# Two sets of modulation dot products in a two-layer diffusion trunk: the latent tokens' change engines, the context's change stage

## The chip, the cores and the metric

The kernel runs on one core of one Trainium2 chip. The metric is the device time of one execution in microseconds (us). Three runs of the kernel before took 1449.05, 1447.75 and 1448.95 us; the median is 1448.95. Five engines work side by side, each through its own instruction queue in order: TensorE (PE, with its weight loads as PEld), VectorE (DVE), ScalarE (ACT), GpSimd (POOL) and SyncE (SP). SP issues all the transfers of this kernel.

## What is computed

There are 1024 latent tokens and 256 context tokens of 1024 numbers each, and two layers. Layer 0 is a windowed attention with grouped keys and values, layer 1 a neighbourhood attention on a grid. Every layer modulates its input with a scale and a shift and gates its output; scale, shift and gate come from a conditioning vector, one for the latent tokens (c) and another for the context (c_ctx).

```python
silu_c, silu_cc = jax.nn.silu(c), jax.nn.silu(c_ctx)
h, hc = x, ctx
for i in range(DEPTH):                        # DEPTH = 2
    shift, scale, gate = jnp.split(silu_c @ w_ada[i] + b_ada[i], 3, axis=-1)
    shift_c, scale_c, gate_c = jnp.split(silu_cc @ w_ada[i] + b_ada[i], 3, axis=-1)
    u = h * (1.0 + scale[:, None, :]) + shift[:, None, :]
    uc = hc * (1.0 + scale_c) + shift_c
    y, yc = mixer_a(...) if i == 0 else mixer_b(...)      # (o * silu(g)) @ w_out
    h = layer_norm(ALPHA * h + gate[:, None, :] * y, ln_g[i], ln_b[i])
    if i < DEPTH - 1:
        hc = layer_norm(ALPHA * hc + gate_c * yc, ln_g[i], ln_b[i])
return h
```

What the change touches are three products of a vector with a 1024 x 1024 matrix, for both vectors: the gate of layer 0 and the shift and scale of layer 1. They are needed only after the first attention: the gates when the output projection's result is gated, shift and scale when the second layer's input u is made.

## The kernel before, in words

**Stages.** Up to about 100 us the first layer's input is modulated and its keys and values are projected. From there to about 590 us the first attention runs over eight head pairs p (some 61 us each), with the projections of the same pair's gate path and the next pair's queries as filling between its steps. The output projection follows to about 697 us, with the first layer norm and the second layer's input, ten blocks b of 128 tokens (0 to 7 latent, 8 and 9 context). Then come the second layer's projections and attention and its output projection. Each float32 product is made of three matmuls on a high part (hi) and a low part (lo = value − hi) of both operands: hi is a cast on ScalarE, lo a subtraction on VectorE or GpSimd.

**The order of work.** The program is written as lists of pieces that `merge` puts together, attention steps with projection pieces. A list scheduler then orders every engine's queue: of the instructions that it takes to be ready it picks the one that stands first in the program. A tile with a tag takes one of the tag's buffers as one comes free; an instruction that needs a buffer waits for the last user of an older tile. `keep_in_program_order` pins an instruction behind the one written just before it for its engine.

**The dots (L592 to L634).** 48 pieces, `dot_half(h, j)` for half h of the 1024 inputs and group j of 128 outputs (j 0 to 7 gate, 8 to 15 shift, 16 to 23 scale), are put evenly into the steps of the first seven head pairs (`SEG`, L41; L819). A piece first gives ScalarE the previous piece's sum (`dot_sum`, pinned in program order). Then it loads 128 x 512 weights (tile gw, 256 KB, two buffers), multiplies and sums them with the latent vector in one VectorE instruction (L617, into the scratch tile gj, which has the tag ra, one buffer, together with the rotary evacuation and the gate's tanh), and multiplies them with the context's vector on GpSimd (L618), in place. That product's sum is the ScalarE instruction L599. Each half starts with both vectors spread over 128 partitions (gh), with silu made of a tanh on ScalarE and an operation on VectorE. `dots_end` (L623) adds the halves and the bias and makes colA and colB, the columns that turn the normalised z into u.

**The attention's tail (p = 7, L824 to L848).** The output projection's weights are loaded and split there (`wo_piece`, tags whi and wlo of the pool wp, four buffers each), block 0 is projected, and `gate_rows` spreads both gates over the partitions (eight transposes and one copy each, tile gates).

**The output projection (L854 to L918).** Before the loop `w.split(NA + 4)` (L858) loads the first four weight tiles of the second layer and splits them. A weight tile takes a raw buffer (wr, tag wraw, two buffers), and a hi and a lo buffer (tags whi and wlo). `og_load` takes the same two raw buffers for each block's attention output (ogr, two halves); `og_split` makes its hi on ScalarE (L385) and its lo on VectorE (L386). For block b the loop loads the residual z, splits og of b, loads ogr of b + 1, issues the block's 48 matmuls (yA), and then `u_from` of the block before: eight transposes of its z on TensorE (uT), eight operations on VectorE (ut, one buffer, two halves), the cast uBh on ScalarE (L887) and the subtraction uBl on GpSimd (L888). After that stand the gate product (L908), the residual (L909), statistics, the root on GpSimd (L429, rsd), and z on ScalarE (L915), which is stored (zdd, blocks 0 to 7) and transposed one block later. Behind the loop the second layer's projections begin (L942), with the weights that `w.split` has made and u of all eight latent blocks.

Of the kernel before, what the change touches and what calls it, by code (L numbers as in the profile page):

```python
# [43 lines left out]
def f32(ap):  # L44
    return ap.bitcast(F32)
# [37 lines left out]
def build(tc, i, out):  # L83
# [13 lines left out]
    def psbig(name):  # L97
        return ps.tile([P, 1024], F32, tag="big", bufs=2, name=name)
# [264 lines left out]
    def gate_rows(dst, src):  # L363

        pg = psbig("gate")
        for j in range(KT):
            nc.tensor.transpose(pg[:, j * P : (j + 1) * P], src[:, j : j + 1].to_broadcast([P, P]), ident)
        nc.scalar.copy(dst, pg)
# [222 lines left out]

    dhalf = cp.tile([P, 24, 2], F32, name="dhalf")  # L592
    gh, sums = [], []
# [7 lines left out]
    def dot_half(h, j):  # L601
        def run():
            dot_sum()
            if j == 0:
                gh.clear()
                for v in range(2):
                    t = px.tile([P, 512], F32, tag=f"gh{v}", bufs=1, name="gh")
                    dma(t, bass.AP(i["cr"].tensor, v * D + h * 512, [[0, P], [1, 512]]))
                    th = px.tile([P, 512], F32, tag="gw", bufs=2, name="gth")
                    nc.scalar.activation(th, t, AF.Tanh, scale=0.5)  # L610
                    nc.vector.scalar_tensor_tensor(t, th, 1.0, t, ALU.add, ALU.mult)
                    gh.append(t)
# [4 lines left out]
            nc.vector.tensor_tensor_reduce(o, t, gh[0], 0.5, 0.0, ALU.mult, ALU.add, accum_out=acc[:, j, 0:1])  # L617
            nc.gpsimd.tensor_tensor(t, t, gh[1], ALU.mult)  # L618
            sums.append((t, acc[:, j, 1:2]))

        return (0.0, run, 0)

    def dots_end():  # L623
        dot_sum()
        for v in range(2):
            d = dcol[:, 0:24, v]
            nc.vector.tensor_tensor(d, d, dhalf[:, 0:24, v], ALU.add)
            nc.vector.tensor_tensor(d, d, bad[:, 16:40], ALU.add)
            shift, scale = dcol[:, 8:16, v], dcol[:, 16:24, v]
            nc.vector.scalar_tensor_tensor(colA[:, v, :], scale, 1.0, lnc[:, 0, :], ALU.add, ALU.mult)  # L630
            nc.vector.scalar_tensor_tensor(colB[:, v, :], scale, 1.0, lnc[:, 1, :], ALU.add, ALU.mult)
            nc.vector.tensor_tensor(colB[:, v, :], colB[:, v, :], shift, ALU.add)

    dots = [dot_half(h, j) for h in range(2) for j in range(24)]  # L634
# [175 lines left out]
    for p in range(8):  # L810
# [6 lines left out]
        if p < 7:  # L817
# [3 lines left out]
            if not dots:  # L821
                att.append((0.0, dots_end, 0))
            merge(att, gprojA(p) + qprojA(p + 1), lead=0.0)
        else:  # L824
# [20 lines left out]
            for v in range(2):  # L845
                gate_rows(gts[:, v], dcol[:, 0:8, v])
# [11 lines left out]
    w.split(NA + 4)  # L858
# [30 lines left out]

    pend = None  # L890
    for b in range(10):
        z = oa.tile([P, D], F32, tag="z", bufs=2, name="z")
        dma(z, i["htok"][b])
        if b == 0:
            yh = yA0
        else:
            o = og_split(up, raw, "h2") if b % 2 else og_split(oa, raw, "og")
            if b < 9:
                raw = og_load(0, b + 1)
            y = psbig(f"yA{b}")  # L900
# [17 lines left out]
        pend = (b, z)  # L918

# [419 lines left out]
```

## Time and profile before

| what | value |
|---|---|
| median of three runs | 1448.95 us |
| the profiled execution | 1450.25 us |
| its span, first to last instruction | 1448.5 us |
| TensorE's granted clock | 0.994 |
| one gw load, from issue to landing | 2.8 us |
| tanh of gh on ScalarE, 4 times | 633 ns |
| bytes moved, over the whole span | 195 MB, 135 GB/s |

The profile is of one execution. A row of the timeline has start, duration, engine, line, operation, what it writes and reads, its size and, in brackets, how long the engine had been idle before it and which instruction released it. A row of a group has, behind the count, the busy time and the mean in nanoseconds, or the lowest, median and highest duration. A row of waits has who waited for whom, the microseconds in total, how many times, and the longest. A row of stretches has start and end, length, and each engine's busy time with its number of instructions, then the clock, the DMA share and GB/s. SPq rows are transfers as SP issues them; "landing" counts from issue to the data's arrival.

### The profile page before, as it was taken

The page shows a single profiled execution, that of the slowest core. Times are in us where ns is not written, and L with a number is a line of the kernel's source. Part 1 is how long each engine was busy: PE and PEld are TensorE (multiplying, and loading weights), DVE is VectorE, ACT ScalarE, POOL GpSimd, SP SyncE. Part 2 cuts the span into 40 slices and gives each one's busy share as a digit, 9 for nine tenths or more (in the row PEclk, how much of TensorE's full clock was granted, in tenths as well). Part 3 has the DMA queues.
Part 4 walks back from the last instruction along what each step waited for, and adds up shares of the span by engine and source line. Part 5 has one row for each costly group of instructions (what it writes and reads, how often), then busy time and mean ns, then how long its engine had stood idle before and what let it go on. Part 6 is the DMA issues. An engine that isn't in the chain of part 4 may idle for free. (4 is left out here: it accounts for less than half of the span.)

```text
span 1448.5 us, 25148 instructions
## 1 busy us (share of the span) xinstructions
PE 1393.6 (96%) x8815; PEld 1217.2 (84%) x8816; DVE 988.8 (68%) x2216; ACT 733.9 (51%) x1561; POOL 631.7 (44%) x779
## 2 busy tenths in 40 slices
PE   8998999999999999999999999999999999998995
PEld 5887888888888888788888899888988898887775
DVE  4658887878888789566423766555565565667698
ACT  4336776677676778332222545554454444557310
POOL 0326666666666657233301333333233333336664
PEclk9999999999999999999999999999999999999998
DMA  9472114123222124434278565565555564384353
GB/s 369 172 227 85 60 48 131 45 77 101 68 70 62 56 67 131 133 129 136 75 216 230 156 195 152 150 166 146 168 147 152 146 182 140 102 207 151 114 133 93
DMA packets 117229, 195.05 MB, mean 135 GB/s; under 512 B 9328, under 2 KB 57840, under 8 KB 117104
## 3 DMA queue, kind: packets, MB, share of 16 engines
q1 hardware_dynamic: 117104, 193.45, 44.4%
q8 instruction: 70, 1.15, 0.3%
q14 instruction: 55, 0.45, 0.1%
HBM read 141.51 MB, written 51.90 MB: 134 GB/s over the span
## 5 line engine op out<-in xcount | busy, mean ns | idle before, releaser
L329 POOL TENSOR_SCALAR s_B<-s_B,rs_B 128x640 f32<-128x640 f32 (+1 forms) x128 | 101.1, 790 | 298.0 <-DVE rs_B L328 243.9
L208 PE MATMUL pj<-uBh,wh 128*128 128x512 f32 (+1 forms) x448 | 176.0, 393 | 0.0
L209 PE MATMUL pj<-uBl,wh 128*128 128x512 f32 (+1 forms) x448 | 170.3, 380 | 0.0
L210 PE MATMUL pj<-uBh,wl 128*128 128x512 f32 (+1 forms) x448 | 170.1, 380 | 0.0
L324 ACT ACTIVATE s_B<-s_B,m_B 128x640 f32<-128x640 f32 (+1 forms) x128 | 102.9, 804 | 131.2 <-DVE m_B L317 131.1
L324 ACT ACTIVATE s_A<-s_A,m_A 128x641 f32<-128x641 f32 (+2 forms) x160 | 119.5, 747 | 88.7 <-DVE m_A L317 73.7
L164 POOL TENSOR_TENSOR wl<-wr,wh 128x512 fp32r<-128x512 f32 x64 | 87.7, 1370 | 162.1 <-ACT wh L162 139.8
L329 POOL TENSOR_SCALAR s_A<-s_A,rs_A 128x640 f32<-128x640 f32 (+2 forms) x160 | 126.8, 793 | 58.0 <-DVE rs_A L328 55.7
L317 DVE CUSTOM_DVE_ANT_0 s_A<-S_A,msk,nsk 128x640 f32<-128x640 f32 (+2 forms) x160 | 123.6, 774 | 34.1 <-PE S_A L705 17.7
L342 DVE TENSOR_TENSOR pt_B<-T_B,pt_B 128x640 fp32r<-128x640 f32 (+1 forms) x128 | 100.9, 788 | 61.0 <-ACT pt_B L340 60.6
L208 PE MATMUL pj<-uAh,wh 128*128 128x512 f32 (+1 forms) x384 | 140.0, 365 | 0.0
L209 PE MATMUL pj<-uAl,wh 128*128 128x512 f32 (+1 forms) x384 | 137.8, 359 | 0.0
L210 PE MATMUL pj<-uAh,wl 128*128 128x512 f32 (+1 forms) x384 | 137.5, 358 | 0.0
L342 DVE TENSOR_TENSOR ptl_A<-T_A,pth_A 128x640 fp32r<-128x640 f32 (+2 forms) x160 | 114.0, 713 | 15.3 <-PE pvA L733 7.1
L336 PE MATMUL T_A<-ident,s_A 128*128 128x128 f32 x672 | 101.1, 275 | 12.2 <-DVE m_A L317 8.9
L336 PEld LDWEIGHTS T_A<-ident,s_A 128*128 128x128 f32 x672 | 77.2, 140 | 40.2 <-issue 16.7
L340 ACT CAST pt_B<-T_B 128x640 fp32r<-128x640 f32 (+1 forms) x128 | 84.3, 658 | 47.6 <-PE T_B L336 46.6
L317 DVE CUSTOM_DVE_ANT_0 s_B<-S_B,bias 128x640 f32<-128x640 f32 (+1 forms) x128 | 100.4, 784 | 10.5 <-PE S_B L1036 9.7
L340 ACT CAST pth_A<-T_A 128x640 fp32r<-128x640 f32 (+2 forms) x160 | 96.4, 603 | 16.8 <-PE T_A L336 14.1
L210 PEld LDWEIGHTS pj<-uBh,wl 128*128 128x128 f32 x448 | 84.3, 188 | 16.6
L336 PE MATMUL T_B<-ident,s_B 128*128 128x128 f32 x608 | 88.7, 275 | 9.9 <-DVE pt_B L342 5.0
L242 PE MATMUL pv<-wh,uBh 128*128 128x256 f32 x320 | 92.8, 291 | 3.1 <-ACT wh L162 3.1
(219 smaller groups left out, 3883.6 us busy)
## 6 DMA issues: line engine op xcount, KB each, us to landing
kB<-kdB SPq DMA_DIRECT2D x64, 320.0 KB, 5.2
gw<-in_wadaT SPq DMA_DIRECT2D x48, 256.0 KB, 2.8
vdB<-st SPq DMA_DIRECT2D x20, 512.0 KB, 3.2
vB<-vdB SPq DMA_DIRECT2D x16, 640.0 KB, 4.7
wada<-in_wadaC SPq DMA_DIRECT2D x16, 512.0 KB, 9.6
kdB<-st SPq DMA_DIRECT2D x16, 512.0 KB, 3.0
qdB<-st SPq DMA_DIRECT2D x16, 512.0 KB, 3.5
qB<-qdB SPq DMA_DIRECT2D x32, 256.0 KB, 4.7
```

The source lines that it names most:

```text
L164: e.tensor_tensor(lo, r, f32(hi), ALU.subtract)
L208: mm(pt[:, :n], hi[:, sl], rh, start=kt == 0, stop=False)
L209: mm(pt[:, :n], hi[:, sl], rl, start=False, stop=False)
L210: mm(pt[:, :n], lo[:, sl], rh, start=False, stop=kt == KT - 1)
L242: mm(pt, lh, hi[:, sl], start=kt == 0, stop=False)
L317: nc.vector.tensor_tensor_reduce(outp, sc, in1, scale, init if init is not None else 3e38, ALU.add, ALU.min, accum_out=s.m)
L324: nc.scalar.activation(s.t[:, :n], s.t[:, :n], AF.Exp, bias=s.m, scale=-1.0, accum_out=s.sum)
L329: nc.gpsimd.tensor_scalar(s.t[:, : s.w], s.t[:, : s.w], s.rs, 1.0, ALU.mult, ALU.mult)
L336: nc.tensor.transpose(tp[:, k * P : (k + 1) * P], s.t[:, src * P : (src + 1) * P], ident)
L340: nc.scalar.copy(pt.hi[:, :n, hl, :], tv)
L342: nc.vector.tensor_tensor(pt.lo[:, :n, hl, :], tv, f32(pt.hi[:, :n, hl, :]), ALU.subtract)
```

## The change

The dots become one piece for each vector v. The latent vector's 48 (v = 0) stay at their places in the attention, but the product is made on GpSimd and the sum on ScalarE; the VectorE instruction and its scratch tile are gone. The context's 48 (v = 1) go into the output projection's loop: six at block 0, and for blocks 1 to 7 two ahead of each half of the block's matmuls and two behind its z. Their tiles come from the pool wp, the vector (gh) under the tag whi, the weights (and the tanh) under wlo. `dots_end` is called for the context's gates when 32 of the 48 are issued and for its shift and scale after the last. The context's gates are spread at the end of block 7, in two halves through one-bank PSUM tiles. `w.split(NA + 4)` moves from ahead of the loop to the beginning of block 8.

```diff
-    def dot_half(h, j):
-        def run():
-            dot_sum()
...
-            acc = dhalf if h else dcol
-            t = px.tile([P, 512], F32, tag="gw", bufs=2, name="gw")
-            dma(t, i["wadaT"][j, :, h * 512 : (h + 1) * 512])
-            o = ap_.tile([P, 512], F32, tag="ra", bufs=1, name="gj")
-            nc.vector.tensor_tensor_reduce(o, t, gh[0], 0.5, 0.0, ALU.mult, ALU.add, accum_out=acc[:, j, 0:1])
-            nc.gpsimd.tensor_tensor(t, t, gh[1], ALU.mult)
-            sums.append((t, acc[:, j, 1:2]))
+    def dot_half(pl, v, h, j):
+
+        dot_sum()
+        if (v, h) not in gh:
+            t = pl("gh", 1)
+            dma(t, bass.AP(i["cr"].tensor, v * D + h * 512, [[0, P], [1, 512]]))
+            th = pl("gw", 2)
+            nc.scalar.activation(th, t, AF.Tanh, scale=0.5)
+            nc.vector.scalar_tensor_tensor(t, th, 1.0, t, ALU.add, ALU.mult)
+            gh[v, h] = t
+        t = pl("gw", 2)
+        dma(t, i["wadaT"][j, :, h * 512 : (h + 1) * 512])
+        nc.gpsimd.tensor_tensor(t, t, gh[v, h], ALU.mult)
+        sums.append((t, (dhalf if h else dcol)[:, j, v : v + 1]))
...
-            for v in range(2):
-                gate_rows(gts[:, v], dcol[:, 0:8, v])
+            gate_rows(gts[:, 0], dcol[:, 0:8, 0])
...
-    w.split(NA + 4)
...
+    late = [(1, h, j) for h in range(2) for j in range(24)]
+
+    def late_tile(x, n):
+        return f32(wp.tile([P, 512], F32R, tag="whi" if x == "gh" else "wlo", bufs=4, name=x))
+
+    def late_dots(n):
+        for _ in range(n):
+            dot_half(late_tile, *late.pop(0))
+            if len(late) == 16:
+                dots_end(1, slice(0, 8))
+            elif not late:
+                dots_end(1, slice(8, 24))
+
     for b in range(10):
+        if b == 0:
+            late_dots(6)
+        elif b == 8:
+            w.split(NA + 4)
         z = oa.tile([P, D], F32, tag="z", bufs=2, name="z")
...
             for sl in HALVES:
+                if b < 8:
+                    late_dots(2)
                 out_part(yh, sl, o, woA, range(KT))
...
         pend = (b, z)
+        if 0 < b < 8:
+            late_dots(2)
+        if b == 7:
+            gate_rows(gts[:, 1], dcol[:, 0:8, 1], True)
```

More of the change, by code (lines that the diff above doesn't have):

```diff
@@ L361, in wo_piece, with gate_rows @@
         e.tensor_tensor(lo, r, f32(hi), ALU.subtract)
[L363 to L368, printed above, removed]
+    def gate_rows(dst, src, halves=False):
+        for n in range(2 if halves else 1):
+            pg = psone("gate") if halves else psbig("gate")
+            for j in range(KT // 2 if halves else KT):
+                k = KT // 2 * n + j
+                nc.tensor.transpose(pg[:, j * P : (j + 1) * P], src[:, k : k + 1].to_broadcast([P, P]), ident)
+            nc.scalar.copy(dst[:, HALVES[n]] if halves else dst, pg)
     def og_load(l, b, n=KT):
@@ L592, in build @@
     dhalf = cp.tile([P, 24, 2], F32, name="dhalf")
-    gh, sums = [], []
+    gh, sums = {}, []
     def dot_sum():
@@ L623, in dots_end @@
-    def dots_end():
-        dot_sum()
[L625 to L632, printed above, removed]
@@ L635, in build @@
+    dots = [(0.0, lambda h=h, j=j: dot_half(lambda x, n: px.tile([P, 512], F32, tag=x, bufs=n, name=x), 0, h, j), 0) for h in range(2) for j in range(24)]
     evs = []
@@ L821, in build @@
             if not dots:
-                att.append((0.0, dots_end, 0))
+                att.append((0.0, lambda: dots_end(0, slice(0, 24)), 0))
             merge(att, gprojA(p) + qprojA(p + 1), lead=0.0)
```

21 lines of the change are left out of this document (10 added, 11 removed).

## The prediction

> **What bounds the kernel now.** I read the page's engine shares first, then the busy time by stretches, then what TensorE waits for.
>
> ```profile
> span 1448.5 us, 25148 instructions
> PE 1393.6 (96%) x8815; PEld 1217.2 (84%) x8816; DVE 988.8 (68%) x2216; ACT 733.9 (51%) x1561; POOL 631.7 (44%) x779
> 222.00:283.00 61.00, 58.61 (x383) 51.09 (x382) 50.68 (x122) 42.94 (x99) 39.96 (x58) 1.00 0.26 81
> 600.00:697.00 97.00, 95.98 (x455) 79.30 (x456) 64.34 (x135) 30.22 (x55) 30.62 (x40) 1.00 0.38 125
> ```
>
> The third line is one head pair of the first attention (span, then PE, PEld, DVE, ACT, POOL), the fourth the output projection with its layer norm. TensorE is busy nearly throughout: 2.4 us idle in the 61, 1.0 in the 97. So time is gained only where TensorE waits, and any new wait of TensorE is paid in full. In the attention VectorE is the second engine (50.68 of 61, 83%); in the output projection GpSimd (30.62 of 97, 32%) and ScalarE (31%) have room. TensorE's waits while the dots run, 100 to 527 us:
>
> ```profile
> PE T_A L336 <- DVE m_A L317: 5.7, 11, 1.6
> PE S_A L704 <- DVE ptl_A L342: 5.1, 7, 1.2
> PE S_A L705 <- DVE ptl_A L342: 1.8, 6, 0.3
> PE T_A L336 <- POOL gw L618: 1.3, 1, 1.3
> ```
>
> Together 13.9 us, 12.6 of them on VectorE: that is all that a lighter VectorE can give in this stage.
>
> **The change part by part.** First, the latent dots leave VectorE (L617).
>
> ```profile
> L617 DVE CUSTOM_DVE_ANT_0 gj<-gw,gh 128x512 f32<-128x512 f32 x48 | 38.1, 794 | 1.4 <-DMA gw<-in_wadaT 1.0
> 249.21 1.52 DVE L617 CUSTOM_DVE_ANT_0 gj<-gw,gh 128x512 f32<-128x512 f32 x1 [0.46 <-DMA gw<-in_wadaT]
> 251.70 0.74 PE L336 MATMUL T_A<-ident,s_A 128*128 128x128 f32 x5 [1.16 <-DVE m_A L317]
> 372.24 1.46 DVE L617 CUSTOM_DVE_ANT_0 gj<-gw,gh 128x512 f32<-128x512 f32 x1 [0.53 <-DMA gw<-in_wadaT]
> 374.66 0.74 PE L336 MATMUL T_A<-ident,s_A 128*128 128x128 f32 x5 [1.16 <-DVE m_A L317]
> 125.29 0.74 PE L336 MATMUL T_A<-ident,s_A 128*128 128x128 f32 x5 [1.30 <-POOL gw L618]
> 280.34 0.39 PE L704 MATMUL S_A<-kA,qA 128*128 128x256 f32 x1 [0.67 <-DVE ptl_A L342]
> ```
>
> 48 reductions, 38.1 us of VectorE, go. GpSimd and ScalarE keep 48 products and 48 sums here, for the other vector. What TensorE gets back is far less than 38.1: the gaps at 251.70 and 374.66 stand right behind reductions of 1.52 and 1.46 us, and at 125.29 it waited for a product that itself waited for its reduction. That is 1.16 + 1.16 + 1.30 = 3.6 us for certain. Of the other 13.9 − 3.6 = 10.3 us I take the dots' share of VectorE's work, 38.1 in seven stretches of 50.68 (11%): 1.1. Gain 4.7 us; the bounds are 0 (work only leaves) and 13.9.
>
> Second, the context's 48 dots come into the output projection, each a load, a product on GpSimd and a sum on ScalarE:
>
> ```profile
> L618 POOL TENSOR_TENSOR gw<-gw,gh x48: 1262/1290/1306, 115.0 to 523.8; 128x512 f32<-128x512 f32 x48
> L599 ACT ACTIVATE gw<-gw x48: 613/632/648, 116.3 to 525.2; 128x512 f32<-128x512 f32 x48
> L599 ACT ACTIVATION_READ_ACCUMULATOR gw<-gw x48: 184/188/207, 116.8 to 525.7; 128x1 f32 x48
> ACT gw L599: 5.8, 9
> ```
>
> 48 × 1.29 = 62 us of GpSimd and 48 × 0.82 = 39 us of ScalarE. Six dots belong to each of blocks 0 to 7. The first ten (blocks 0 and 1, before the waits on block 1's normalisation) have the attention's tail for cover; if that is gone they join the queue below. A sum that waits for its product holds ScalarE's queue, the og casts and uBh behind it; in the attention that happened to 9 of 48, 5.8 us in all (last row), and ScalarE's 31% leaves room for it. The context's two tanh and their products, and the two VectorE steps that end its dots, move along; the last of these waits for dot 47's sum, with block 8's z behind it on VectorE, a microsecond that the wait ahead of block 9 (below) covers: nothing; 1 us if that wait is gone. One block's period, from one uBl to the next, with what stands in it:
>
> ```profile
> 675.45 1.44 POOL L888 TENSOR_TENSOR uBl<-ut,uBh 128x256 fp32r<-128x256 f32 x2 [5.23 <-ACT uBh L887]
> 678.81 1.90 POOL L888 TENSOR_TENSOR uBl<-ut,uBh 128x256 fp32r<-128x256 f32 x2 [1.92 <-ACT uBh L887]
> 681.47 0.55 POOL L429 TENSOR_TENSOR rsd<-rsd,half 128x1 f32<-128x1 f32 x1 [0.76 <-DVE rsd L428]
> 687.52 1.45 POOL L888 TENSOR_TENSOR uBl<-ut,uBh 128x256 fp32r<-128x256 f32 x2 [5.50 <-ACT uBh L887]
> 690.89 1.44 POOL L888 TENSOR_TENSOR uBl<-ut,uBh 128x256 fp32r<-128x256 f32 x2 [1.92 <-ACT uBh L887]
> 682.29 1.24 ACT L915 ACTIVATE z<-z,rsd 128x1024 f32<-128x1024 f32 x1 [3.25 <-issue]
> 684.30 1.04 PE L869 MATMUL uT<-ident,z 128*128 128x128 f32 x8
> 685.10 0.47 PE L419 MATMUL yA<-woAh,og 128*128 128x512 f32 x1
> 696.11 1.03 PE L869 MATMUL uT<-ident,z 128*128 128x128 f32 x8
> 679.40 0.70 DVE L386 TENSOR_TENSOR og<-ogr,og 128x512 fp32r<-128x512 f32 x1
> 680.14 1.11 DVE L386 TENSOR_TENSOR og<-ogr,og 128x512 fp32r<-128x512 f32 x1
> ```
>
> GpSimd has 1.44 + 1.90 + 0.55 = 3.9 us in a period of 12.07; six products add 7.74: 11.6, 96%. The chain from a block's last matmul to its transposes (uT) passes GpSimd twice, at the first uBl (the second half of ut has the same buffer) and at rsd; z ends at 683.53, 0.77 ahead of the transposes that read it. A product is in GpSimd's way 7.74/12.07 = 64% of the time and then by half of 1.29: 0.41 us a passage, 0.82 for two. That is about what the slack covers on average, so it costs something only when they bunch. In such a chain the loss is between 0 and, if two whole products stand in the way each time, 2 × 1.29 − 0.77 = 1.8 a block, 11 over blocks 2 to 7. I take 0.5 a block, 3 us, near the lower end: VectorE's statistics can be queued ahead of the late ut half.
>
> The second og subtraction took 1.11 where the first took 0.70, and it began while GpSimd's uBl was still running. The Trainium skill ("SBUF — State Buffer", SBUF: two separate sides) says that GpSimd and a VectorE operation with two SBUF inputs share one port pair, and whoever starts first shuts the other out for its whole instruction. These two rows agree. By that rule each product could also hold up the two og subtractions ahead of rsd.
>
> Third, the split of the second layer's first four weight tiles (four loads, casts, subtractions) moves from ahead of the loop to block 8. The rows of the raw buffers' queue:
>
> ```profile
> 571.36 2.55 SPq L148 DMA_DIRECT2D wr<-in_wBk  x2
> 576.71 0.33 SPq L148 DMA_DIRECT2D wr<-in_wBq  x1
> 578.48 0.33 SPq L148 DMA_DIRECT2D wr<-in_wBq  x1
> 581.30 3.67 SPq L375 DMA_DIRECT2D ogr<-ogd  x2
> 668.37 1.52 SPq L375 DMA_DIRECT2D ogr<-ogd  x2
> 672.47 1.14 ACT L385 CAST og<-ogr 128x512 fp32r<-128x512 f32 x2 [0.73 <-PE yA L421]
> DMA to landing us min/median/max: 2.5/2.9/6.3
> L162 ACT CAST wh<-wr x18: 604/620/625, 574.7 to 793.4; 128x512 fp32r<-128x512 f32 x18
> L164 POOL TENSOR_TENSOR wl<-wr,wh x9: 1285/1293/1298, 575.4 to 791.4; 128x512 fp32r<-128x512 f32 x9
> L164 DVE TENSOR_TENSOR wl<-wr,wh x9: 680/693/1369, 577.5 to 794.9; 128x512 fp32r<-128x512 f32 x9
> ```
>
> The tag wraw has two buffers, for wr and ogr alike, and they are given in program order: four wr, and only then the next block's ogr (581.30). Under the cover of the attention's tail that cost nothing. After the change the four wr stand between block 8's ogr and block 9's, which now loads at 668.37 for matmuls at 685.10. The pace of the old place (571.36 to 581.30, 9.9 us) would still do: 668.37 + 9.9 + 2.9 + 0.62 = 681.8. But a wr gives its buffer back only when its low half is written, and the low halves (wlo, four buffers) wait for the last dots to be summed. The sums of dots 45 and 46 are pinned behind block 7's z, that of 47 behind them. So: z ends at 683.53; the three sums end at 684.35, 685.17 and 685.99 (0.82 each). The third weight tile's low half on GpSimd then ends at 685.17 + 1.29 = 686.5 and frees the first buffer for ogr; it lands at 689.4 (2.9) and is cast by 690.0 (0.62). TensorE, which could start at 685.10, waits 4.9 us. The other half: 684.35 + 0.69 (VectorE) = 685.0, the fourth wr lands at 687.9, cast 688.6, low half 689.3, ogr 692.2, cast 692.8; the first half's twelve matmuls last until 690.0 + 12 × 0.23 = 692.8 (block 9's 48 take the 11.0 us from 685.10 to 696.11), so nothing more. Nothing else is ready for TensorE: the second layer's projection needs block 7's uBl, which ended at 690.89 + 1.44 = 692.3 even without the products. Cost 4.9; bounds 0 (as in the old place) and 4.9 + 3 × 1.29 = 8.8, if the last three products are late too.
>
> What moves at no cost: the context's gate rows (8 transposes and copies) go from the tail to block 7; TensorE does the same work. Each of the 48 loads is issued by the SP queue ahead of the ogr, z and zdd transfers there; at 38% DMA share, and with ogr loaded about 4 us (668.37 against the cast at 672.47) and its matmuls 17 us ahead, I take none of it.
>
> Sum, against the profiled execution's own 1450.25 us: − 4.7 + 3 + 4.9 = + 3.2, 1453.45. The median of the runs, 1448.95, lies 1.3 below that execution; the forecast is 1452.1 us. A measurement of this kernel tells about 0.2%, 2.9 us, from no change: this is just over it.
>
> **The rivals.**
> *VectorE's queue was the cause of all attention waits* (faster). Then 13.9 goes instead of 4.7: 1442.9. It decides from a gain of 10.8 on (3 + 4.9 + 2.9). For it: 12.6 of 13.9 us end on VectorE. Against: gaps like that at 280.34 have no reduction right ahead of them.
> *No wait ahead of block 9*, the wlo buffers being free in time: 1448.95 − 4.7 + 3 = 1447.2, no change that can be told, or a little faster. Against: the pinned sums behind z.
> *GpSimd's order becomes the bound* (slower still): if all six products stand between rsd and the next uBl, a period is uBl's start to rsd's end (675.45 to 682.02, 6.6) + 7.74 = 14.3, 2.2 over 12.07, for six blocks 13.4 instead of 3: 1462.5. It decides where the products come in one bunch.
> *The port lock*: two og subtractions each held by a product, as the second one above was by uBl (1.11 − 0.70 = 0.41), on top of the two passages: 4 × 0.41 − 0.77 = 0.9 a block, 5.2 for six instead of 3: 1454.3. By the rule of the Trainium skill cited above it would go this way.
>
> **How the numbers follow.** Forecast 0.40 (slower 0.24, same 0.14, faster 0.02: it lies at the border); VectorE alone 0.20 (faster 0.19, same 0.01); no wait 0.20 (same 0.12, faster 0.07, slower 0.01); GpSimd's order 0.10 and the lock 0.10 (slower 0.19, same 0.01). Sum: faster 0.28, same 0.28, slower 0.44. Each of the first three terms can reach its bound, so the range goes from the VectorE rival, 1443, to near the GpSimd rival, 1460; the forecast's own range is 1448 to 1457.
>
> **What would show it.** Right: no reductions on VectorE between 100 and 527 us and TensorE's waits there down by about 5 of 13.9; GpSimd over 80% busy from 600 to 685; TensorE idle some 5 us ahead of block 9's matmuls, released by the og cast, with four wr loads between block 8's and 9's ogr. Wrong: TensorE unbroken from block 8 to the second layer (no wait), or uT waiting a microsecond or more for z in most blocks (GpSimd's order).

## The result and the profile after

| what | before | after |
|---|---|---|
| median | 1449.0 us (4 runs, 1447.75 to 1449.66) | 1493.61 us (4 runs, 1493.29 to 1498.86) |
| ratio, with 95% interval | | 1.0323 (1.0307 to 1.0338) |
| profiled execution, span | 1450.25, 1448.5 us | 1493.74, 1492.0 us |

The change costs 3.2%. The forecast was 1452.1 us with a range up to 1460: the sign that had the largest chance was right, the size was wrong by more than a factor of ten. Line numbers of the changed kernel differ: uT is L865, ut L873, uBh L883, uBl L884, og L387 and L388, rsd L431 (GpSimd) and L930 (VectorE), z L931, a product L616, a sum L602, a load of gw L615.

Two stretches of after, the head pair and the output projection that the prediction showed:

```profile
222.00:283.00 61.00, 57.74 (x383) 51.09 (x381) 45.77 (x110) 43.17 (x102) 39.35 (x59) 1.00 0.25 77
600.00:697.00 97.00, 80.33 (x340) 64.90 (x339) 54.77 (x107) 40.73 (x99) 59.48 (x58) 0.91 0.59 191
```

In the head pair VectorE has 4.9 us less to do, and TensorE does no more for it (57.74, before 58.61). In the output projection TensorE has gone from 1.0 us idle to 16.7, and GpSimd, twice as busy as before, still works only 61% of the time. It is not full; something else holds the stage. What TensorE waits for between 527 and 800 us, after:

```profile
PE uT L865 <- ACT z L931: 21.3, 6, 4.6
PE yA L421 <- ACT og L387: 4.7, 1, 4.7
PE yA L423 <- DVE og L388: 4.0, 1, 4.0
```

The first row is what the prediction named as the sign against itself: uT waits for z, in most blocks. The start of each block's transposes gives the account. Before they began at 601.02, 612.68, 624.49, ... 684.30, 696.11, 713.85; after at 609.64, 620.28, 635.83, 651.87, 668.35, 686.69, 704.60, 720.11, 744.51, 762.25.

| stretch | change of the span, us |
|---|---|
| attention, up to the last store of its seventh head pair (544.06 to 540.97) | −3.1 |
| the attention's tail and block 0, up to the first uT | +11.7 |
| first to eighth uT, seven periods (83.28 to 110.47) | +27.2 |
| eighth to ninth uT (11.81 to 24.40) | +12.6 |
| ninth to tenth uT (17.74 in both) | 0 |
| the rest, behind the tenth uT (734.65 to 729.75) | −4.9 |
| sum | +43.5 |

Of the last −4.9, 2.5 is one wait in the second layer (pv for a weight cast): 3.1 us in the profiled execution of before, 0.6 in that of after.

**One block.** The timelines of both kernels from one uT to the next, cut to the chain that leads from the one to the other. First before:

```profile
648.36 1.03 PE L869 MATMUL uT<-ident,z 128*128 128x128 f32 x8
651.09 0.71 ACT L887 CAST uBh<-ut 128x256 fp32r<-128x256 f32 x2 [1.35 <-DVE ut L877]
651.58 1.44 POOL L888 TENSOR_TENSOR uBl<-ut,uBh 128x256 fp32r<-128x256 f32 x2 [5.24 <-ACT uBh L887]
...
657.58 0.55 POOL L429 TENSOR_TENSOR rsd<-rsd,half 128x1 f32<-128x1 f32 x1 [0.76 <-DVE rsd L428]
658.16 0.16 DVE L914 SCALAR_TENSOR_TENSOR rsd<-mv,rsd 128x1 f32<-128x1 f32 x1 [0.73 <-POOL rsd L429]
658.40 1.24 ACT L915 ACTIVATE z<-z,rsd 128x1024 f32<-128x1024 f32 x1 [3.24 <-issue]
```

Then after, with what stands between:

```profile
651.87 1.09 PE L865 MATMUL uT<-ident,z 128*128 128x128 f32 x8 [1.08 <-ACT z L931]
...
654.07 0.63 ACT L602 ACTIVATE gw<-gw 128x512 f32<-128x512 f32 x1
...
655.21 0.71 ACT L883 CAST uBh<-ut 128x256 fp32r<-128x256 f32 x2
656.20 1.29 POOL L616 TENSOR_TENSOR gw<-gw,gh 128x512 f32<-128x512 f32 x1 [2.53 <-DMA gw<-in_wadaT]
657.45 1.44 POOL L884 TENSOR_TENSOR uBl<-ut,uBh 128x256 fp32r<-128x256 f32 x2
...
662.51 1.54 POOL L884 TENSOR_TENSOR uBl<-ut,uBh 128x256 fp32r<-128x256 f32 x2 [1.13 <-ACT uBh L883]
662.67 0.15 DVE L430 TENSOR_SCALAR rsd<-mv 128x1 f32<-128x1 f32 x1
664.02 1.25 POOL L616 TENSOR_TENSOR gw<-gw,gh 128x512 f32<-128x512 f32 x1
665.23 0.54 POOL L431 TENSOR_TENSOR rsd<-rsd,half 128x1 f32<-128x1 f32 x1
665.75 1.25 POOL L616 TENSOR_TENSOR gw<-gw,gh 128x512 f32<-128x512 f32 x1
665.81 1.22 DVE L930 SCALAR_TENSOR_TENSOR rsd<-mv,rsd 128x1 f32<-128x1 f32 x1 [2.99 <-POOL rsd L431]
...
667.06 1.24 ACT L931 ACTIVATE z<-z,rsd 128x1024 f32<-128x1024 f32 x1 [1.03 <-DVE rsd L930]
...
668.35 1.04 PE L865 MATMUL uT<-ident,z 128*128 128x128 f32 x6 [4.48 <-ACT z L931]
```

The path is a closed loop: uT, first half of ut, uBh, uBl (which frees the one ut buffer), second half of ut, statistics, rsd, z, and the next uT. Before it takes 3.22 us from uT to uBl, 6.00 to rsd, 0.82 to z and 2.03 to the next uT: 12.07. After: 5.58, 7.78, 1.83, 1.29, together 16.48. The 2.36 of the first leg are uBh 0.61 later (sums and casts of og stand ahead of it on ScalarE) and uBl 1.75 later still: a product that waits for its load stands ahead of it on GpSimd. In the second leg rsd is ready to start at 662.82 and starts at 665.23, behind the second uBl and a product. The third leg is new: a VectorE step of one number per partition takes 1.22 us instead of 0.16 while a product runs. Over the ten blocks this step took 1.21 to 1.24 us three times, 0.70 once and 0.16 or less in the others, so the legs differ from block to block. The 0.74 taken back in the last leg is all the slack there was.

### The profile page after: what moved, and what is told of

Same layout as the page of the kernel before. It is cut to its first block, busy times and chain, and to the rows that moved or that the text cites. A ratio compares the mean times of both kernels' runs of the same rounds, so it can differ in the third digit from the quotient of the medians.

```text
span 1492.0 us, 25264 instructions
## 1 busy us (share of the span) xinstructions
PE 1407.9 (94%) x8816; PEld 1226.8 (82%) x8816; DVE 962.9 (65%) x2122; ACT 764.4 (51%) x1658; POOL 681.2 (46%) x827
## 5 line engine op out<-in xcount | busy, mean ns | idle before, releaser
L616 POOL TENSOR_TENSOR gw<-gw,gh 128x512 f32<-128x512 f32 x96 | 125.7, 1314 | 65.3 <-DMA gw<-in_wadaT 59.7
L329 POOL TENSOR_SCALAR s_A<-s_A,rs_A 128x640 f32<-128x640 f32 (+2 forms) x160 | 120.6, 755 | 54.9 <-DVE rs_A L328 44.1
L210 PEld LDWEIGHTS pj<-uBh,wl 128*128 128x128 f32 x448 | 84.3, 188 | 16.7
```

The lines of the kernel that those rows point to most:

```text
L210: mm(pt[:, :n], lo[:, sl], rh, start=False, stop=kt == KT - 1)
L329: nc.gpsimd.tensor_scalar(s.t[:, : s.w], s.t[:, : s.w], s.rs, 1.0, ALU.mult, ALU.mult)
L616: nc.gpsimd.tensor_tensor(t, t, gh[v, h], ALU.mult)
```

## The experiments

**The parts alone.** *The latent part* leaves the context's late dots out and puts the split and the gate rows back:

```diff
     w.cap = len(srcs)
+    w.split(NA + 4)
...
-        if b == 0:
-            late_dots(6)
-        elif b == 8:
-            w.split(NA + 4)
```

> The context's 48 dots (loads, products, sums) are left out, so the context's gate, shift and scale are the bare bias; the latent dots are on GpSimd and ScalarE in the attention as changed, the split and both gates stand where they stood before. If the loss comes from the context's dots, it is gone and what the attention gained is left: the last store of the seventh head pair was 3.1 us earlier (540.97 against 544.06 us), so about 1446 us. If the attention gains nothing, 1449. If VectorE had been the cause of all its waits, 1435.

Measured: 1444.31 us, ratio 0.9973 (0.9962 to 0.9983), so −4.0 us. The gain is there, at about its expected size. Where it comes from is told below.

*The split alone* is the kernel before, with this edit:

```diff
     w.cap = len(srcs)
-    w.split(NA + 4)
...
     for b in range(10):
+        if b == 8:
+            w.split(NA + 4)
```

> The kernel before, with nothing but the split of the second layer's first four weight tiles moved to block 8. If the wait ahead of block 9 needs both, the raw buffers' order and low buffers that are held by dots, the split's 9.9 us pace fits: 1449 us, no wait of TensorE ahead of block 9. If the raw buffers' order alone makes it, TensorE waits there as in the changed kernel, 4.7 and 4.0 us, and with the slow clock behind the gaps the time is about 1460.

Measured: 1454.05 us, ratio 1.0038 (1.0025 to 1.0051), +5.5 us; neither side had it. The raw buffers go in the order foretold (wr from 668.29 and 673.56, ogr from 678.87), and no matmul of block 9 waits for og. The cost comes by another way, in this timeline:

```profile
676.84 0.62 ACT L162 CAST wh<-wr 128x512 fp32r<-128x512 f32 x1 [3.90 <-DMA wr<-in_wBq]
...
678.25 0.71 ACT L886 CAST uBh<-ut 128x256 fp32r<-128x256 f32 x2
...
687.69 1.97 PE L868 MATMUL uT<-ident,z 128*128 128x128 f32 x8 [3.30 <-ACT z L916]
```

A weight cast waits on ScalarE for its load (3.90 us), with uBh behind it in the queue, and uT, 15.5 us after the one before, waits for z. This was the first sight of the pattern: an instruction off the loop waits for a transfer, and one on the loop stands behind it.

**What in the late dots costs.** Six variants of the changed kernel. *No load*: the late products multiply the resident vector by itself, in place of the weights. *Not pinned*: late sums are free of program order. *Neither*: both. *All behind z*: six dots behind each z. *Own buffers*: six gw tiles in other memory, and the split back in its place. *Two ut*: the second half of ut gets its own buffer.

```diff
# no load
+        if v:
+            nc.gpsimd.tensor_tensor(t, gh[v, h], gh[v, h], ALU.mult)
...
# not pinned
+            if v == 0:
+                tc.keep_in_program_order(s)
# all behind z
-                if b < 8:
-                    late_dots(2)
...
-            late_dots(2)
+            late_dots(6)
# two ut
+            ut = own[:, 0].rearrange("p (k t) -> p k t", k=4) if hf and b < 8 else oa.tile([P, 4, P], F32, tag="ut", bufs=1, name="ut")
```

> The changed kernel, where the context's dots load no weights (the product is of the resident vector with itself, out of place): 48 products and 48 sums of the same size, in the same order and buffers, are left. If the blocks are late because products wait in GpSimd's queue for their loads, the waits of the transposes for z fall from 21.3 us to a few and the time to about 1465 (the wait ahead of block 9 stays). If GpSimd's added 62 us or the port is what costs, the waits stay and the time is 1485 or more.

> The changed kernel, with the context's sums no longer pinned in program order. If the loop from z over the pinned sums, the buffers and the loads to the products is what makes the blocks late, it opens: waits of the transposes under 10 us, 1465 to 1475. If the products' place ahead of uBl and rsd in GpSimd's queue is enough whatever frees the buffers, or GpSimd's capacity, the time stays near 1490.

> The changed kernel, where the context's dots load no weights (resident vector times itself) and their sums are not pinned: both waits of the loop are out, the 48 products and 48 sums are left. If waiting is all that costs, what remains is the moved split (5.8 us by its own run) on a kernel that gained 4: 1450 to 1455, transposes waiting under 5 us. If 62 us more of products in GpSimd's queue cost by themselves, it stays near the 1473 and 1475 of the single removals.

> The changed kernel, with all six dots of blocks 1 to 7 written behind the block's z, none ahead of its matmuls. If the products' place in the program ahead of uBl and rsd is what costs, the transposes' waits fall by half or more: 1465 to 1475. If the loop through the four buffers and the pinned sums decides, it stays at 1485 to 1495, as every sum now stands behind a z.

> The changed kernel, with the context's tiles in room of their own (six weight buffers and two for the vector, in the space that the second layer's context part takes only after block 8) and the split back ahead of the loop; positions and pinned sums as changed. If the four shared buffers made the loads late, the products wait for few of them and, with no wait ahead of block 9, the time is 1450 to 1460. If the products' and sums' places do it with any number of buffers, transposes still wait 10 us or more: 1470 to 1480.

> The changed kernel, with a second buffer for the second half of ut in blocks 0 to 7, so that VectorE's second half of ut, and the statistics behind it, no longer wait for the first uBl on GpSimd: the loop passes GpSimd once (rsd) instead of twice. If products ahead of uBl are what lengthens the blocks, a good part of the 27 us of blocks 1 to 7 goes: 1470 to 1482. If the products ahead of rsd, or the loads alone, are what counts: 1490 or more.

| variant | median us | ratio (95%) | uT's waits for z, us | tail | seven periods | ahead of block 9 |
|---|---|---|---|---|---|---|
| before | 1449.0 | | 1.4 | 57.0 | 83.3 | 11.8 |
| as changed | 1493.61 | 1.0323 (1.0307 to 1.0338) | 21.3 | 68.7 | 110.5 | 24.4 |
| no load | 1473.21 | 1.0170 (1.0157 to 1.0183) | 11.8 | 59.0 | 97.3 | 24.0 |
| not pinned | 1475.36 | 1.0186 (1.0170 to 1.0202) | 18.4 | 73.3 | 99.1 | 11.8 |
| neither | 1466.28 | 1.0126 (1.0105 to 1.0146) | 13.5 | 65.9 | 94.6 | 11.9 |
| all behind z | 1497.15 | 1.0340 (1.0325 to 1.0355) | 27.5 | 64.8 | 113.2 | 29.5 |
| own buffers | 1487.57 | 1.0271 (1.0256 to 1.0287) | 24.8 | 57.5 | 124.3 | 12.5 |
| two ut | 1484.38 | 1.0250 (1.0225 to 1.0276) | 19.1 | 68.0 | 103.2 | 21.3 |

The last three columns are microseconds in each kernel's profiled execution: from the last store of the seventh head pair to the first uT, from there to the eighth uT, and from there to the ninth. Apart from *all behind z*, which came out near its worse side, no variant fitted either side of its expectation in full.

Without loads the tail is 9.7 us shorter and the seven periods 13.2: waiting for loads is one cost. The size isn't clean, because a product of the resident vector with itself also takes less, 1.04 us in the middle instead of 1.29. Without pins the periods are 11.3 shorter and the wait ahead of block 9 is gone, but the tail is 4.6 longer. More buffers don't cure it: with six tiles of their own the periods are longer than as changed, and what this kernel gains lies outside them, where the split is back as well. A second ut buffer, which takes one of the loop's two passages of GpSimd out, makes the periods 7.3 shorter.

With loads and pins gone 1.26%, 18 us over the kernel before, still stays, 8.9 of it in the tail and 11.3 in the periods of the profiled execution. One period of 20.5 has 8.7 of these: there a VectorE subtraction of og, which takes 0.6 to 1.1 us in the blocks behind, took 5.40 (629.91 to 635.31), while GpSimd ran four products, two uBl and two products more, one behind the other. In the kernel with pins but no loads the products come in bunches, here ahead of the first uBl of a block (its timeline):

```profile
638.83 1.97 PE L868 MATMUL uT<-ident,z 128*128 128x128 f32 x8 [3.09 <-ACT z L934]
639.47 6.59 POOL L616 TENSOR_TENSOR gw<-gh 128x512 f32<-128x512 f32 x6 [0.98 <-ACT gw L602]
646.02 1.44 POOL L887 TENSOR_TENSOR uBl<-ut,uBh 128x256 fp32r<-128x256 f32 x2
```

From the second on its periods up to the eighth uT are 14.0 to 15.4 us: about the 14.3 that the rival of GpSimd's order gave, and above the 13.2 that it gives with this kernel's 6.59 us for six products (6.6 + 6.59).

**Is it TensorE's slower clock?** After each wait of 4 us the granted clock is down, 0.93 on average from 650 to 700 us. Seventeen matmuls that nobody reads, ahead of uT in blocks 2 to 7, keep TensorE from idling:

```diff
+            if 1 < b < 8:
+                wps = psone("fill")
+                for _ in range(17):
+                    tc.keep_in_program_order(mm(wps, o[0][0], woA.at(0, HALVES[0])[0], start=True, stop=True))
             u_from(*pend)
```

> The changed kernel, with 17 matmuls of no use (3.9 us) between block b's matmuls and the transposes of the block before, for blocks 2 to 7, where TensorE waits 1 to 4.6 us. If the halved clock behind the gaps comes from the gaps, it stays at full speed there, and the time falls by about 2.5 us for each of five gaps, to about 1481. If the clock falls for another reason, or the waits only grow with the work, 1493 or more.

Measured: 1497.83 us, ratio 1.0338 (1.0313 to 1.0363). From 650 to 700 us TensorE is busy 48.5 of 50 us and its clock is 1.00:

```profile
650.00:700.00 50.00, 48.54 (x224) 39.68 (x223) 25.21 (x50) 19.43 (x49) 31.37 (x30) 1.00 0.54 174
```

The time is not less: the seven periods take 116.3 us, 110.5 without the filling. But the run can't tell by itself what a full clock is worth, because the filling costs TensorE about as much as it could give: 17 matmuls at 0.23 us, the block's own 48 (11.0) and uT (0.8) are 15.7 us, and the three periods from the second uT on are 15.6 to 16.0. What speaks against the clock as the cost of these blocks is read from the changed kernel itself: ahead of six uT TensorE had done its matmuls, slow ones included, and stood waiting for z, up to 4.61 us. There TensorE doesn't set the period; of the slow clock only the transposes stand in the loop, 1.97 us for eight at most instead of 1.04. Ahead of block 9 it is different (below).

**Place or work?** The kernel before, with products of 1.29 us added to each of blocks 1 to 7, on data in SBUF, that nobody reads. First one and three of them pinned ahead of the first uBl:

```diff
+                if 0 < b < 8 and hf == 0 and c == 0:
+                    for _ in range(3):
+                        tc.keep_in_program_order(nc.gpsimd.tensor_tensor(own[:, 2], own[:, 0], own[:, 1], ALU.mult))
...
```

> The kernel before, with one more GpSimd product (128x512, on data that lies in SBUF: no load, no sum, nobody reads it) pinned ahead of the first uBl in each of blocks 1 to 7. If a block is a closed loop of about 11.3 us in a period of 12.07, one product of 1.29 us lengthens the period by 1.29 - 0.77 = 0.5 us: 7 blocks, 3.6 us, ratio about 1.0025. If TensorE sets the period and products only use GpSimd's spare time: no change, 1449 us.

> As the one before, with three such products ahead of the first uBl. Closed loop: 3.87 - 0.77 = 3.1 us a block, 22 us in all, about 1471 us, with uT waiting some 3 us for z in every block from 2 on. If the prediction's cost for waiting behind products (0.5 us a block) held for six products: at most 3 us, 1452.

Measured: 1449.99 us, ratio 1.0015 (1.0005 to 1.0026), and 1450.11 us, ratio 1.0011 (1.0000 to 1.0022). The loop theory's 22 us for three didn't come. But the three products were not where they were meant to be: GpSimd had nothing else to do behind rsd and ran them there, from 659.08 to 663.11, with the next uBl at 665.31 (timeline with three):

```profile
658.57 0.55 POOL L429 TENSOR_TENSOR rsd<-rsd,half 128x1 f32<-128x1 f32 x1 [0.69 <-DVE rsd L428]
659.08 4.03 POOL L892 TENSOR_TENSOR own<-own 128x512 f32<-128x512 f32 x3
659.15 1.24 DVE L921 SCALAR_TENSOR_TENSOR rsd<-mv,rsd 128x1 f32<-128x1 f32 x1 [0.66 <-POOL rsd L429]
```

The same rows explain what they did cost, and why one costs as much as three: the first product holds VectorE's 128x1 step for 1.24 us instead of 0.16, and 1.08 − 0.77 of slack is 0.3 a block, 2 us in seven. The Trainium skill ("SBUF — State Buffer", SBUF: two separate sides) says that the loser on the port pair of VectorE and GpSimd is shut out for the winner's whole instruction; this trace agrees, 1.24 beside a product of 1.29.

So the pair was repeated with products that read ut, and can't start before it is written:

```diff
-  nc.gpsimd.tensor_tensor(own[:, 2], own[:, 0], own[:, 1], ALU.mult)
+  nc.gpsimd.tensor_tensor(own[:, 2], own[:, 0], ut.rearrange("p k t -> p (k t)"), ALU.mult)
```

> The kernel before, with one GpSimd product (128x512) ahead of the first uBl of blocks 1 to 7 that reads the first half of ut, so that it can't start before ut is written and stands between ut and uBl. Place is what counts: the first uBl comes about 0.8 us later (it can start while ScalarE makes uBh), which is the slack of 0.77: 0 to 3 us over the kernel before. Work is what counts: as the product behind rsd, 0.15%.

> Three such products. Place: the first uBl comes 0.8 + 2 x 1.29 = 3.4 us later, less 0.77 of slack is 2.6 a block, 18 us in seven blocks, ratio about 1.0125, with uT waiting for z in most blocks. Work: as three products behind rsd, 0.1%.

Measured: one, 1450.53 us, ratio 1.0013 (0.9999 to 1.0027); three, 1462.58 us, ratio 1.0096 (1.0076 to 1.0116), +14 us where the expectation had 18. The timeline with three:

```profile
642.02 1.09 PE L871 MATMUL uT<-ident,z 128*128 128x128 f32 x8 [0.18 <-ACT z L922]
644.52 4.36 POOL L892 TENSOR_TENSOR own<-own,ut 128x512 f32<-128x512 f32 x3 [4.08 <-DVE ut L879]
648.84 1.45 POOL L893 TENSOR_TENSOR uBl<-ut,uBh 128x256 fp32r<-128x256 f32 x2
...
656.26 1.08 PE L871 MATMUL uT<-ident,z 128*128 128x128 f32 x4 [2.25 <-ACT z L922]
```

uBl comes 6.82 us behind uT instead of 3.22, VectorE takes 0.70 of the 3.60 back by doing an og subtraction and half of the statistics first, 0.74 is slack: 2.2 a block. The same three products cost 0.1% in one place and 1.0% in the other: place, not work.

**Off the loop.** Four versions put dots where the loop isn't. *Behind rsd*: all 48 late, eight of them in the tail and five a block, in five tiles of their own loaded ahead of the block's matmuls, the products of these five pinned behind rsd, sums behind z without a pin, two ut, split in its old place. *Gates stay*: the sixteen gate pieces as before the change, the context's other 32 late, four a block. *Off the loop*: only twenty late, three a block in two sets of tiles; sums pinned behind the second uBh; the 128x1 step made on GpSimd ahead of the products. *Off but held*: the same with that step on VectorE.

```diff
         mv, rs = ln_stats(oa, st)
+        nc.vector.tensor_scalar(mv[:, 1:2], mv[:, 0:1], -1.0, None, ALU.mult)
+        tc.keep_in_program_order(nc.gpsimd.tensor_tensor(rs[:, 0:1], mv[:, 1:2], rs[:, 1:2], ALU.mult))
+        for t, h, j in loaded[:3]:
+            tc.keep_in_program_order(nc.gpsimd.tensor_tensor(t, t, own[6 + h], ALU.mult))
...
-        nc.vector.scalar_tensor_tensor(rs[:, 0:1], mv[:, 0:1], -1.0, rs[:, 1:2], ALU.mult, ALU.mult)
```

> The latent dots as changed, the split of the weights back ahead of the loop, and the context's dots with their own space: five weight tiles, loaded a block ahead; their products pinned behind rsd, where GpSimd has nothing to do for the loop until the next uBl; their sums behind z without a pin; two buffers for ut. 48 dots: 16 under the attention's tail and in block 0, then five a block. If it is the place in the in-order queues that costs, and not GpSimd's or ScalarE's work, most of the 44 us goes and the attention's 4.0 stay: 1445 to 1452. If the added work itself can't be hidden beside the output projection: 1465 or more, as with the loads left out or the pins left out.

> The kernel before, with the sixteen gate pieces as they were; the 32 latent shift and scale dots on GpSimd and ScalarE in the attention, without VectorE; the context's 32 in the output projection, four a block, in four tiles of their own: products pinned behind rsd, sums behind z, next loads behind the store of z. The split stays ahead of the loop. Place is the cause: two thirds of the attention's 4.0 us and next to nothing lost, 1445 to 1449. Work is the cause: 32/48 of the 27 us in the blocks, 18 us, so 1463 or more.

> As the version with the gates left in place, but only the last twenty context dots are late, three a block in blocks 1 to 7, in six tiles (two sets, loaded a block ahead); the sums are pinned behind the second uBh instead of z; and the 128x1 product between rsd and z is made on GpSimd, ahead of the three products, instead of on VectorE beside them. If uBh's delay and the held 128x1 step are the whole of the loss, the blocks are back at 12.0 to 12.1 us and the attention gives 20/48 of 4.0: 1446 to 1448.5. If any three products a block cost what four did: 1455 or more.

> The same, with the 128x1 step left on VectorE, where it starts while GpSimd has just begun the first of three products. If GpSimd's product holds it for the product's length, the step takes 1.2 us instead of 0.16 and z comes 1.07 later, less the 0.77 of slack: 0.3 a block, 2 us more than the other version. If not held: the same time.

Measured, in this order: 1475.78 us, ratio 1.0186 (1.0166 to 1.0207); 1464.98, 1.0111 (1.0094 to 1.0129); 1458.56, 1.0063 (1.0046 to 1.0079); 1461.78, 1.0077 (1.0058 to 1.0096). The first three missed the side of their expectation on which place is all that costs, and each trace showed another queue.

Behind rsd, SP was held: these are three rows of its queue, where the loads of the dots wait for their tiles and z and ogr stand behind them. One period took 31 us.

```profile
620.59 8.03 SPq L905 DMA_DIRECT2D ownh<-in_wadaT  x4
628.71 0.38 SPq L935 DMA_DIRECT2D z<-in_htok  x1
...
632.71 6.91 SPq L377 DMA_DIRECT2D ogr<-ogd  x3
```

With the gates left in place the blocks took 13.7 us: four sums stood on ScalarE from 646.91 to 650.14, uBh started 4.02 us after uT instead of 2.73, and the 128x1 step was held (1.23 us). With both mended three of the seven still took 14.0 (the others 11.6 to 12.7), because SP now put the store of z ahead of the second ogr, and the og cast waited for its load with uBh behind it (677.11):

```profile
669.43 0.38 SPq L375 DMA_DIRECT2D ogr<-ogd  x1
671.60 0.33 SPq L946 DMA_DIRECT2D zdd<-z  x1
...
672.02 0.39 SPq L375 DMA_DIRECT2D ogr<-ogd  x1
...
676.58 0.62 ACT L385 CAST og<-ogr 128x512 fp32r<-128x512 f32 x1 [1.89 <-DMA ogr<-ogd]
```

The pair that differs only in the 128x1 step is inconclusive by its times (the intervals overlap), though the rows show 1.21 to 1.25 us against 0.19 on GpSimd. In the profiled executions its seven periods took 93.9 us against 90.3, the way that was expected, but the attention differed by 2.4 us the other way. The last three of the four also had an attention 2.5 to 5.5 us longer than before; why the mixed pieces do that wasn't followed.

The last kernel leaves the attention as before and makes twenty of the context's dots a second time, beside the output projection, with all three queues in order and the 128x1 step on GpSimd:

```diff
-            dma(zdd[b * P : (b + 1) * P, :], z)
+            tc.keep_in_program_order(dma(zdd[b * P : (b + 1) * P, :], z))
...
+            tc.keep_in_program_order(dma(t, i["wadaT"][j, :, h * 512 : (h + 1) * 512]))
```

> The kernel before with its attention untouched, and twenty of the context's dots made a second time beside the output projection, three a block in blocks 1 to 7, off the loop in every queue: products on GpSimd behind the step that makes the bias of z, sums on ScalarE behind the second uBh, and on SP the store of z pinned behind the loads of ogr, the loads of the dots behind the store. If the order in the three queues is all that the work cost, twenty dots cost nothing beside the projection: 1448 to 1451, blocks of 12.0 to 12.2 us. If not: 1455 or more, as with the version before, and what holds the blocks stays open.

Measured: 1449.93 us, ratio 1.0006 (0.9994 to 1.0017): nothing that can be told from no change. A block of its timeline:

```profile
657.45 1.53 SPq L375 DMA_DIRECT2D ogr<-ogd  x2
...
659.31 0.19 POOL L932 TENSOR_TENSOR rsd<-mv,rsd 128x1 f32<-128x1 f32 x1
659.45 2.54 POOL L934 TENSOR_TENSOR ownh<-ownh,ownl 128x512 f32<-128x512 f32 x2
659.53 1.25 ACT L937 ACTIVATE z<-z,rsd 128x1024 f32<-128x1024 f32 x1 [1.37 <-POOL rsd L932]
660.80 0.33 SPq L939 DMA_DIRECT2D zdd<-z  x1
```

uT starts at 649.51 and 661.58: 12.07, as before. Twenty loads, products and sums, three a block, cost nothing here, where none of them stands ahead of the loop in any queue and the 128x1 step is out of their way. That all 48 could be had so wasn't tried, and no version that does the whole computation beat the kernel before.

## Why the prediction was wrong

**The attention's gain (term 1, −4.7): right in size, wrong in place, so the size was luck.** The latent part alone gives −4.0. The prediction put 2.3 of it at the two gaps at 251.70 and 374.66 and thought the waits of all seven stretches would shrink. They did so only in the first: TensorE's waits from 100 to 179 us fell from 5.3 to 2.0 us, and from 179 to 527 rose from 9.2 to 11.3, without making that stretch longer (365.2 us from the first pair's store to the seventh's before, 364.9 after). Together they fell by 1.2 us, where the prediction's sign asked for about 5. The stretch around the one gap that was right (125.29), before and then after:

```profile
124.00:148.00 24.00, 20.59 (x127) 17.53 (x128) 20.23 (x47) 16.93 (x39) 16.13 (x22) 1.00 0.18 56
```

```profile
124.00:148.00 24.00, 23.23 (x146) 19.96 (x146) 17.47 (x43) 16.49 (x39) 17.48 (x25) 1.00 0.15 50
```

TensorE does 2.6 us more work in the same 24. Why waits for VectorE cost time there and not in the later pairs, where it is as busy (20.23 of 24 here, 50.68 of 61 there), wasn't tried.

**The products beside the output projection (term 2, +3): the step that failed.** "A product is in GpSimd's way 7.74/12.07 = 64% of the time and then by half of 1.29" counts a product only while it executes. In an in-order queue it is in the way from the moment it is next, and in this kernel it was next while its load was on the way: from 545 to 745 us products waited 34.7 us for their loads and sums 49.4 us for their products. The loads were late because their tiles waited for sums (SP waited 40.6 us for sums ahead of loads, 540 to 800), sums pinned behind z, and z waits for the loop: the delays feed on each other. The prediction had the loop's two passages of GpSimd and its 0.77 of slack right, but took the slack as cover for an average, put nothing for ScalarE ("leaves room for it"), nothing for SP ("I take none of it"), and went near the lower end because VectorE's statistics "can be queued ahead of the late ut half"; where that was measured, with three products on the loop, it gave back 0.70 of 3.60. GpSimd, forecast to be over 80% busy from 600 to 685 us, was busy 61%. The blocks paid 27.2 us.

**Its rivals.** GpSimd's order, given 0.10, named the right mechanism, and its period of 14.3 is near what the blocks show once nothing waits for a load. It lacked the wait for loads, up to some 20 us, and so its 1462.5 was still far short. The port lock was looked for at the og subtractions. In the changed kernel they took 1.3 to 2.8 us a block, 1.9 on average, against 1.8 in every block before, so on balance they cost nothing there; the 5.40 us in the kernel with neither loads nor pins shows that they can. What was held in the changed kernel is, in three blocks, the 128x1 step ahead of z, for a whole product.

**The tail ("the attention's tail for cover", nothing): wrong.** The tail and block 0 took 11.7 us longer. ScalarE's sums wait there for products (9.8 us between 560 and 601) that wait for loads (8.2), with casts of the attention behind them. The price was foreseen as joining "the queue below"; that queue was what cost. Without loads the same stretch took only 2.1 us longer.

**The moved split (term 3, +4.9): the mechanism right, the sum too small.** The timeline of after, at block 9:

```profile
720.58 1.27 POOL L164 TENSOR_TENSOR wl<-wr,wh 128x512 fp32r<-128x512 f32 x1 [2.78 <-ACT gw L602]
...
721.88 0.38 SPq L377 DMA_DIRECT2D ogr<-ogd  x1
...
725.22 0.62 ACT L387 CAST og<-ogr 128x512 fp32r<-128x512 f32 x1 [1.33 <-DMA ogr<-ogd]
725.89 0.80 PE L421 MATMUL yA<-woAh,og 128*128 128x512 f32 x1 [4.75 <-ACT og L387]
...
730.34 0.68 DVE L388 TENSOR_TENSOR og<-ogr,og 128x512 fp32r<-128x512 f32 x1
...
731.07 0.79 PE L423 MATMUL yA<-woAh,og 128*128 128x512 f32 x1 [3.96 <-DVE og L388]
```

Step by step as worked out: the pinned sum, the low half, the buffer, ogr, the cast, and a wait of 4.75 us where 4.9 was forecast. The variants bear it out: with the pins gone this stretch takes 11.8 us as before, with only the loads gone still 24.0. But "so nothing more" was wrong twice. The third matmul waits 3.96 us more for the low part of the same half of og, which the sum left out: VectorE makes it behind the second half of ut, which waits for uBl, and the statistics. And the granted clock is 0.50 from 731 to 737 us: the matmuls start 0.43 us apart instead of 0.23, and the block's 48 take about 3.7 us longer beside that wait. In all the stretch lost 12.6. Alone, the split costs 5.5 us by the loop instead, which the prediction's bound of 0 ("as in the old place") left out.

**The range.** Its upper end lay near the GpSimd rival's, and below what the prediction's own bounds add up to (no gain, 11 and 8.8: 1468.8); no bound was made for a loop in which every turn waits for a transfer. Six loads of 2.8 us a block, each into a tile that a sum has to set free, were in the profile and in the code.

## What to carry to other kernels

Before putting work into an engine's idle time, find the loop that sets the stage's period and ask of each queue it passes (the engines' and SP's) what will stand ahead of it: an instruction that waits for a transfer blocks all behind it, and its price is its wait, not its duration. A low busy share promises nothing: GpSimd at 32% could take three products a block for nothing at one place and for 2 us a block at another. Pin such work behind the loop's last passage of each queue, load it a turn ahead, and test the place with a dummy that depends on the loop's data; a dummy that doesn't will run somewhere else.

## What the hardware showed

The step that makes z's bias, 128x1 on VectorE, took 0.16 us in all ten blocks of before, and 1.23 or 1.24 in each of blocks 1 to 7 with one GpSimd product of 1.29 us put right behind rsd: the smallest instruction pays for the whole of the other. A 128x512 subtraction on VectorE was held for longer than one instruction: in the kernel with neither loads nor pins it took 4.49 us at 578.83, beside four products run one behind the other (4.04 us from 578.73), and 5.40 at 629.91.

The granted clock fell to half after TensorE's waits. After 4.61 us of waiting eight transposes took 1.97 us instead of 1.04, in the timeline of after:

```profile
704.60 1.97 PE L865 MATMUL uT<-ident,z 128*128 128x128 f32 x8 [4.61 <-ACT z L931]
```

In the kernel with three products on the loop a wait of 2.25 us was enough for a clock of 0.56 to 0.59 over the next 4 us; behind waits of 2.00 (684.72) and 1.74 us (698.75) there it stayed at 1.00. The Trainium skill ("TensorE: Matmul & The Clock Gate", Part 1: The HAM clock gate) gives an idle window of about 3.4 us for this; the 2.25 us row is below it. Where TensorE waits for a chain in every block anyway, the slow matmuls were over before the next wait; ahead of block 9, where nothing was left to wait for, they cost about 3.7 us.
